# A decoder layer with two attentions: probabilities times values in three split passes, one head's transposed probabilities in six slots

## The chip, the cores and the metric

The kernel runs on one core of a Trainium2 chip. The metric is the device time of one launch in microseconds (us); smaller is better.

## What is computed

One layer of a decoder trunk in float32: 512 rows (tokens) of 2048 channels. The part that the change touches is the mixer with two attentions of eight heads each, both with values of 128 columns:

```python
h = rms_norm(x, g_attn) * (1 + sc_a) + sh_a          # sc_a, sh_a from c @ w_ada
proj = h @ w_in                                      # q, k, v, indexer, latents, gates
# mixer A: 8 query heads over 2 key/value heads, 128 keys chosen per row by an indexer
p = softmax(where(valid, qg @ k_sel, -inf));  o_a = p @ v_sel
# mixer B: 8 heads, keys and values from a latent, causal
p = softmax(where(causal, q @ k, -inf));      o_b = p @ v
merged = sigmoid(gate_a) * (o_a @ w_pa) + sigmoid(gate_b) * (o_b @ w_pb)
x = x + gt_a * (merged @ w_o)
x = x + gt_f * conv_ffn(rms_norm(x, g_ffn) * (1 + sc_f) + sh_f)
```

## The kernel before

The 512 rows are four blocks of 128, called tb for rows, qb for queries and kc for keys. Nearly all large products run as **three split passes**: both operands are held as a pair hi + lo in the type float32r, and mm3 (lines 165 to 168) issues hi·hi, hi·lo and lo·hi into one bank. The helper split (lines 152 to 154) makes such a pair: ACT copies the source to hi, and DVE subtracts hi from the source to give lo. Weights come by DMA into the buffer raw and are split into whl (wtile, lines 145 and 146; from line 1090 on by lines 153 and 154).

The small attention products are plain float32 matmuls: queries times keys (line 1023 in mixer A, line 1366 in mixer B beside the split rotary part of line 638) and **probabilities times values** (line 813).

One head goes like this. attend_p, or the loop in attend_pair, fills a bank with the scores of a query block; soft does the softmax on DVE (lines 784, 786, 787) and ACT (785), for qb 3 down to 0. attend_pv then takes the key blocks kc 0 to 3: for each it transposes the probabilities of the query blocks kc to 3 on PE (line 805, 10 transposes per head) into a bank, and copies 512, 384, 256 or 128 columns to SBUF, for even kc on ACT (line 810), for odd kc on DVE (line 808). Four matmuls with these widths add into one bank (line 813), which lines 815 and 816 split into the pair that the next product takes.

SBUF is handed out in 81 slots of 128x512 float32. attend_bufs takes five slots for probabilities and five for their transposes, enough for two heads at once (quad cuts them by the head's number modulo two), and four for outputs. at_bank gives the four PSUM banks 4 to 7 in turn to scores, transposes and outputs.

Beside the attention runs filler work, so that PE has something to do while softmax is under way: in mixer A the gate projections (gate_steps through fill) and a stream of w_ada columns that DVE adds up (lines 856 and 858, after ada_load, which takes two slots a step from those that are free); in mixer B the projection w_pa (pa_block) and the next pair's key, value and query projections (up_pair). After the last pair load_gates runs sigmoids on ACT (lines 1420 and 1421) on gates that it loads.

The program is not run in the order in which it is written: an ordering pass puts each engine's instructions in a row by priority, by a few explicit rules (high_priority, issue_after) and by its own estimate of when operands are ready. On the chip every engine then works through its row in order. So an instruction that waits holds up all that stand behind it on its engine.

## Time and profile before

| | |
|---|---|
| runs | 2595.93, 2594.96, 2591.62 us; median 2594.96 |
| profiled execution | 2592.58 us, of which its span is 2590.8 us |
| PE | 2574.9 us busy, 99% of the span; granted clock 1.000 |
| DVE | 2176.5 us, 84% |
| ACT | 1240.8 us, 48% |
| POOL | 374.7 us, 14% |
| probabilities times values (line 813) | 437 to 595 us (mixer A) and 837 to 992 us (mixer B) |

PE is busy throughout. The end of a matmul record is modelled, and records of consecutive matmuls overlap, so the cost of one in a stream is the step from its start to the next start, not its length. A row of the timeline may merge several records of one line (x10).

### The profile page before, as it was taken

How to read it: one execution, taken by the hardware profiler on the slowest of the kernel's cores; microseconds unless marked ns; L12 is line 12 of the kernel's file. 1: busy time of each engine (PE TensorE's matmuls, PEld its weight loads, DVE VectorE, ACT ScalarE, POOL GpSimd, SP SyncE). 2: the span in 40 equal slices, each digit the busy share in tenths (PEclk: the TensorE clock that was granted, in tenths of full speed). 3: DMA queues.
4: the chain of work that ended last, by engine and by line, in shares of the span. 5: the costliest groups of instructions: out<-in, count | busy, mean ns of one | idle time of the engine just before them, and what ended most of it. 6: DMA issues, size and time to landing. Idle time of an engine off the chain costs nothing.

```text
span 2590.8 us, 45201 instructions
## 1 busy us (share of the span) xinstructions
PE 2574.9 (99%) x17392; PEld 2340.4 (90%) x17392; DVE 2176.5 (84%) x3487; ACT 1240.8 (48%) x1949; POOL 374.7 (14%) x671
## 2 busy tenths in 40 slices
PE   9999999999999999999999999999999999999999
PEld 8887787779998877888889999999999999999999
DVE  7977986788878767876979989999989998989887
ACT  6333444344445535322545555555555555665554
POOL 1000011010023223200100000000000024414120
PEclk9999999999999999999999999999999999999999
DMA  9953136655685579976424334433444358868663
GB/s 342 362 166 103 45 102 203 214 160 170 210 265 168 160 213 347 322 232 225 155 75 158 125 122 137 138 116 132 129 147 137 125 173 229 225 168 226 155 204 116
DMA packets 216444, 466.41 MB, mean 180 GB/s; under 512 B 23930, under 2 KB 65556, under 8 KB 216228
## 3 DMA queue, kind: packets, MB, share of 16 engines
q1 hardware_dynamic: 170404, 344.93, 41.9%
q0 software_dynamic: 45792, 118.59, 15.4%
q8 instruction: 136, 2.23, 0.3%
q14 instruction: 80, 0.66, 0.1%
q10 hardware_dynamic: 32, 0.01, 0.0%
HBM read 398.16 MB, written 65.27 MB: 179 GB/s over the span
## 4 chain that ended last, share of the span: by engine, by line
PE 94%; issue 2%; DMA 2%; DVE 1%; ACT 1%; POOL 0%; SPq 0%; POOLq 0%; ACTq 0%; DVEq 0%
PE bank L1218 18%; PE bank L1220 18%; PE bank L1219 18%; PE bank L166 12%; PE bank L168 12%; PE bank L167 12%; PE bank L813 1%; PE bank L1366 1%; DMA raw<-in_w_ada 1%; PE bank L805 0%; PE bank L349 0%; DMA slot<-in_x 0%; PE bank L638 0%; DMA slot<-in_w_ada 0%; PE bank L1023 0%
## 5 line engine op out<-in xcount | busy, mean ns | idle before, releaser
L1218 PE MATMUL bank<-slot,whl 128*128 128x256 f32 x3920 | 1098.4, 281 | 3.1 <-ACT slot L1099 1.2
L1219 PE MATMUL bank<-slot,whl 128*128 128x256 f32 x3920 | 1097.1, 281 | 0.0
L1220 PE MATMUL bank<-slot,whl 128*128 128x256 f32 x3920 | 1084.9, 281 | 2.2 <-DVE whl L154 2.2
L1218 PEld LDWEIGHTS bank<-slot,whl 128*128 128x128 f32 x3920 | 737.3, 188 | 5.5 <-ACT slot L1099 2.3
L1219 PEld LDWEIGHTS bank<-slot,whl 128*128 128x128 f32 x3920 | 739.2, 189 | 0.2
L1220 PEld LDWEIGHTS bank<-slot,whl 128*128 128x128 f32 x3920 | 731.3, 188 | 2.7 <-DVE whl L154 2.6
L154 DVE TENSOR_TENSOR whl<-raw,whl 128x1024 fp32r<-128x1024 f32 (+2 forms) x560 | 608.0, 1088 | 126.5 <-ACT whl L153 120.8
L153 ACT ACTIVATE whl<-raw 128x1024 fp32r<-128x1024 f32 (+2 forms) x560 | 530.7, 949 | 359.2 <-PE bank L1219 180.2
L145 ACT ACTIVATE whl<-raw 128x1024 fp32r<-128x1024 f32 (+4 forms) x182 | 187.4, 1032 | 361.5 <-PE bank L168 183.1
L1095 DVE TENSOR_TENSOR raw<-raw 128x1024 f32<-128x1024 f32 (+2 forms) x320 | 347.3, 1085 | 3.9 <-DMA raw<-in_w_ups 1.7
L146 DVE TENSOR_TENSOR whl<-raw,whl 128x1024 fp32r<-128x1024 f32 (+4 forms) x182 | 215.7, 1187 | 111.3 <-ACT whl L145 109.8
L167 PE MATMUL bank<-whl,slot 128*128 128x512 f32 (+2 forms) x768 | 295.2, 385 | 0.0
L168 PE MATMUL bank<-whl,slot 128*128 128x512 f32 (+2 forms) x768 | 294.1, 385 | 0.0
L166 PE MATMUL bank<-whl,slot 128*128 128x512 f32 (+2 forms) x768 | 290.1, 389 | 0.8 <-DVE slot L1330 0.7
L167 PE MATMUL bank<-slot,whl 128*128 128x512 f32 (+1 forms) x656 | 263.5, 402 | 0.0
L166 PE MATMUL bank<-slot,whl 128*128 128x512 f32 (+1 forms) x656 | 261.3, 405 | 0.7 <-ACT slot L1548 0.7
L168 PE MATMUL bank<-slot,whl 128*128 128x512 f32 (+1 forms) x656 | 257.5, 401 | 0.0
L1101 ACT ACTIVATE slot<-bank 128x256 f32<-128x256 f32 x192 | 73.6, 383 | 210.9 <-PE bank L1220 210.9
L166 PEld LDWEIGHTS bank<-whl,slot 128*128 128x128 f32 x768 | 144.2, 188 | 30.5 <-issue 2.2
L858 DVE SCALAR_TENSOR_TENSOR slot<-slot,c_act,slot 128x512 f32<-128x512 f32 x203 | 151.0, 747 | 23.2 <-DMA slot<-in_w_ada 21.0
L167 PEld LDWEIGHTS bank<-whl,slot 128*128 128x128 f32 x768 | 144.4, 188 | 28.8 <-issue 2.1
L168 PEld LDWEIGHTS bank<-whl,slot 128*128 128x128 f32 x768 | 144.2, 188 | 28.9 <-issue 1.4
(302 smaller groups left out, 2789.7 us busy)
## 6 DMA issues: line engine op xcount, KB each, us to landing
slot<-in_w_ada SPq DMA_DIRECT2D x344, 256.0 KB, 5.4
raw<-in_w_ups SPq DMA_DIRECT2D x160, 512.0 KB, 3.7
raw<-in_w_in SPq DMA_DIRECT2D x50, 512.0 KB, 3.7
raw<-in_w_down SPq DMA_DIRECT2D x64, 384.0 KB, 4.0
raw<-in_w_down SPq DMA_DIRECT2D x64, 320.0 KB, 4.0
slot<-f POOLq DMA_DIRECT2D x154, 128.0 KB, 4.7
f<-slot POOLq DMA_DIRECT2D x66, 256.0 KB, 5.1
raw<-in_w_gs SPq DMA_DIRECT2D x32, 512.0 KB, 4.5
```

The lines of the kernel that those rows point to most:

```text
L145: A.activation(hi, raw[:, :w], AF.Copy)
L146: last["lo"] = V.tensor_tensor(lo, raw[:, :w], r32(hi), ALU.subtract)
L153: return (A.activation(dst_hi, src, AF.Copy), V.tensor_tensor(dst_lo, src, r32(dst_hi), ALU.subtract))
L154: V.tensor_tensor(dst_lo, src, r32(dst_hi), ALU.subtract))
L166: PE.matmul(o, lh, rh, start=first, stop=False)
L167: PE.matmul(o, lh, rl, start=False, stop=False)
L168: PE.matmul(o, ll, rh, start=False, stop=last)
L858: V.scalar_tensor_tensor(acc, ts[i], c_act[:, k:k + 1], acc, op0=ALU.mult, op1=ALU.add)
L1095: V.tensor_tensor(o[:, :W], a[:, :W], b[:, :W], op)
L1218: PE.matmul(o, wh[:, ks], rh, start=first and k == 0, stop=False, skip_group_check=True)
L1219: PE.matmul(o, wh[:, ks], rl, start=False, stop=False, skip_group_check=True)
L1220: PE.matmul(o, wl[:, ks], rh, start=False, stop=last, skip_group_check=True)
```

## The change

Probabilities times values becomes three split passes too.

- In attend_pv all four copies become split: ACT writes hi and DVE writes lo, for every kc, and the matmul becomes mm3.
- The transposed probabilities lie in three slots for hi and three for lo, of **one** head: quad is called with number 0 for each head. Before, there were five slots for two heads.
- The values are split too. In mixer A, four splits of 128x256 behind the key work of lines 714 to 722, into four new slots (va); the slots kva are given back earlier. In mixer B, line 1295 becomes a split, and vv takes four slots a pair instead of two.

```diff
--- before.py
+++ after.py
@@ -710,6 +710,10 @@
     qaT = {}
     kaT = [get(), get()]
     kva = part["B"][0:4]
+    va = ([getr(), getr()], [getr(), getr()])
+
+    def va_part(e, tb):
+        return va[e][tb // 2][:, (tb % 2) * 256:(tb % 2) * 256 + 256]
 
     for tb in range(4):
         t = kva[tb]
@@ -720,12 +724,14 @@
         rsqrt_mean(r, ss, P, 2)
         V.tensor_tensor(k3, k3, r[:, :, None].to_broadcast([P, 2, P]), ALU.mult)
         rope(k3, 2, 32, "ka", tb)
+        split(va_part(0, tb), va_part(1, tb), t[:, 256:512])
 
     for g in range(2):
         b = at_bank()
         for tb in range(4):
             PE.transpose(b[:, tb * P:(tb + 1) * P], kva[tb][:, g * P:(g + 1) * P], ident)
         A.activation(kaT[g], b, AF.Copy, scale=gk_col)
+    put(*kva)
 
     def ev_qa(cb):
         def ev(tb, b):
@@ -764,10 +770,11 @@
 
     def attend_bufs():
         att["p"] = [get() for _ in range(5)]
-        att["t"] = [get() for _ in range(5)]
+        att["t"] = [getr() for _ in range(3)]
+        att["l"] = [getr() for _ in range(3)]
         att["o"] = [getr() for _ in range(4)]
 
-    def attend_free(kinds="pto"):
+    def attend_free(kinds="ptlo"):
         for k in kinds:
             put(*att[k])
 
@@ -789,28 +796,25 @@
     def attend_p(qk, maskf, nsc, vf, dh, dl):
         i = hcount[0] % 2
         hcount[0] += 1
-        pq, pt = quad(att["p"], i), quad(att["t"], i)
+        pq = quad(att["p"], i)
         for qb in (3, 2, 1, 0):
             S = (qb + 1) * P
             b = at_bank()
             qk(b, qb, S)
             soft(b[:, :S], pq[qb][:, :S], maskf(qb), nsc(qb))
-        return i, pq, pt, vf, dh, dl
-
-    def attend_pv(i, pq, pt, vf, dh, dl):
+        return i, pq, vf, dh, dl
+
+    def attend_pv(i, pq, vf, dh, dl):
+        pt, pl = [quad([*att[n][0:2], None, None, att[n][2]], 0) for n in "tl"]
         for kc in range(4):
             b = at_bank()
             n = (4 - kc) * P
             for qb in range(kc, 4):
                 PE.transpose(b[:, (qb - kc) * P:(qb - kc + 1) * P], pq[qb][:, kc * P:(kc + 1) * P], ident)
-            d = pt[3 - kc]
-            if kc % 2:
-                last["cp"] = V.tensor_copy(d, b[:, :n])
-            else:
-                A.activation(d, b[:, :n], AF.Copy)
+            last["cp"] = split(pt[3 - kc], pl[3 - kc], b[:, :n])[1]
         ob = at_bank()
         for kc in range(4):
-            PE.matmul(ob[:, kc * P:], vf(kc), pt[3 - kc], start=kc == 0, stop=kc == 3)
+            mm3(ob[:, kc * P:], *vf(kc), pt[3 - kc], pl[3 - kc], kc == 0, kc == 3)
         oh, ol = att["o"][2 * i], att["o"][2 * i + 1]
         A.activation(oh, ob, AF.Copy)
         last["ol"] = V.tensor_tensor(ol, ob, r32(oh), ALU.subtract)
@@ -1023,7 +1027,7 @@
                 PE.matmul(o[:, :S], qaT[qb, g][:, (hd % 4) * P:(hd % 4 + 1) * P], kaT[g][:, :S], start=True, stop=True)
 
             state = attend_p(qk, lambda qb: mask[qb], lambda qb, hd=hd: nsc_a[:, qb, hd:hd + 1],
-                             lambda kc, g=g: kva[kc][:, 256 + g * P:256 + (g + 1) * P], *oa_d[hd])
+                             lambda kc, g=g: [va_part(e, kc)[:, g * P:(g + 1) * P] for e in range(2)], *oa_d[hd])
         fill(1, 1)
         if prev:
             attend_pv(*prev)
@@ -1031,7 +1035,7 @@
         prev = state
     fill(26)
     put(*kaT)
-    put(*kva)
+    put(*va[0], *va[1])
     for t in qaT.values():
         put(t)
     put(mslot, tslot[0])
@@ -1280,7 +1284,7 @@
 
     def up_pair(hp):
         kn = [get() for _ in range(2)]
-        vv = [get() for _ in range(2)]
+        vv = [getr() for _ in range(4)]
         kr = get()
         kr3 = kr.rearrange("p (t a d) -> p t a d", t=4, a=2)
 
@@ -1292,7 +1296,7 @@
             b4 = b.rearrange("p (n e d) -> p n e d", n=2, e=2)
             k3 = two(kn, tb)
             A.activation(k3, b4[:, :, 0, :], AF.Copy)
-            V.tensor_copy(two(vv, tb), b4[:, :, 1, :])
+            split(two(vv[0:2], tb), two(vv[2:4], tb), b4[:, :, 1, :])
             ss = sm.tile([P, 2], F32, name="ss2")
             head_ss(ss, k3, tb)
             V.tensor_scalar(ss, ss, ss_kr[:, tb:tb + 1], None, op0=ALU.add)
@@ -1366,7 +1370,7 @@
                 PE.matmul(bs[a][:, :S], qT[a][:, qs], kT[a][:, :S], start=False, stop=True)
                 soft(bs[a][:, :S], pq[a][qb][:, :S], Z[:, 384 - qb * P:512], nsc_b[:, qb, a:a + 1])
         for a in range(2):
-            attend_pv(a, pq[a], quad(att["t"], a), lambda kc, a=a: two(vv, kc)[:, a, :],
+            attend_pv(a, pq[a], lambda kc, a=a: [two(vv[2 * e:2 * e + 2], kc)[:, a, :] for e in range(2)],
                       *(ob_d[hp * 2 + a] if hp < 3 else (None, None)))
         put(*vv)
         put(*kT)
@@ -1390,7 +1394,7 @@
         pa_block(hp)
         if hp < 2:
             up_pair(hp + 2)
-    attend_free("pt")
+    attend_free("ptl")
 
     ada_in_slots[0] = ada_ring_on[0] = True
     ada_ring.extend(get() for _ in range(6))
```

The new rows have the line numbers of the changed file: transposes are L813 there (L805 before), the passes L166 to L168 with a slot on both sides, the copies and subtractions of split L153 and L154, sigmoids L1424 and L1425.

**PE, first pair of mixer B,** the end of the transposes and the start of probabilities times values; L813 below is the product before and the transpose after. Before:

```order
L805 MATMUL bank_73<-ident,slot_7244 128x128
L805 MATMUL bank_73<-ident,slot_7243 128x128
L168 MATMUL bank_68<-whl,slot_6540 128x384
L166 MATMUL bank_66<-whl,slot_446 128x384
L167 MATMUL bank_66<-whl,slot_446 128x384
L168 MATMUL bank_66<-whl,slot_447 128x384
L166 MATMUL bank_67<-whl,slot_6543 128x384
L813 MATMUL bank_70<-slot_7246,slot_6745 128x512
L813 MATMUL bank_70<-slot_7247,slot_6745 128x384
L813 MATMUL bank_70<-slot_7250,slot_6746 128x256
L813 MATMUL bank_70<-slot_7247,slot_6746 128x128
L813 MATMUL bank_71<-slot_7248,slot_6745 128x512
```

After:

```order
L813 MATMUL bank_73<-ident,slot_7356 128x128
L813 MATMUL bank_73<-ident,slot_7355 128x128
L166 MATMUL bank_70<-slot_5106,slot_847 128x512
L167 MATMUL bank_70<-slot_7359,slot_847 128x512
L168 MATMUL bank_70<-slot_5106,slot_852 128x512
L166 MATMUL bank_70<-slot_5107,slot_847 128x384
L167 MATMUL bank_70<-slot_7360,slot_847 128x384
L168 MATMUL bank_70<-slot_5107,slot_852 128x384
L166 MATMUL bank_70<-slot_7358,slot_851 128x256
L167 MATMUL bank_70<-slot_7361,slot_851 128x256
L168 MATMUL bank_70<-slot_7358,slot_6851 128x256
```

Five filler matmuls between the last transposes and the product are gone, and further up those between the transposes: between the last scores (128 columns) and the product there were 44 filler matmuls and are now 3. Behind these rows come the three passes of 128 columns and at once those of the second head.

**DVE, the same place,** from the row that finishes the last probabilities of the first head (128x128; ri is the reciprocal of the row sums). Before:

```order
L787 TENSOR_SCALAR slot_7242<-slot_7242,ri 128x128
L1295 COPY slot_6845<-bank_67 128x256
L1298 TENSOR_SCALAR ss_7528<-ss_7528,ss_kr 128x2
L787 TENSOR_SCALAR slot_7244<-slot_7244,ri 128x128
L707 TENSOR_REDUCE ss_7547<-slot_6726 128x2
L858 SCALAR_TENSOR_TENSOR slot_354<-raw,c_act,slot_354 128x512
L269 TENSOR_SCALAR rsm<-ss_7528 128x2
L1295 COPY slot_6999<-bank_68 128x256
L1298 TENSOR_SCALAR ss_7547<-ss_7547,ss_kr 128x2
L707 TENSOR_REDUCE ss_7566<-slot_6725 128x2
L858 SCALAR_TENSOR_TENSOR slot_354<-raw,c_act,slot_354 128x512
L808 COPY slot_7247<-bank_73 128x128
```

After:

```order
L794 TENSOR_SCALAR slot_7354<-slot_7354,ri 128x128
L154 TENSOR_TENSOR slot_7360<-bank_71,slot_5107 128x384
L793 RECIPROCAL ri<-su 128x1
L1305 TENSOR_TENSOR slot_7213<-slot_7213,rs_7712 128x256
L794 TENSOR_SCALAR slot_7356<-slot_7356,ri 128x128
L146 TENSOR_TENSOR whl<-raw,whl 128x1024
L154 TENSOR_TENSOR slot_7361<-bank_72,slot_7358 128x256
L154 TENSOR_TENSOR slot_7360<-bank_73,slot_5107 128x128
L154 TENSOR_TENSOR slot_7359<-bank_70,slot_5106 128x512
```

The lo parts of the four key blocks stand with a weight subtraction of 1024 columns (L146) among them, and the product waits for the last (512 columns).

**ACT, last pair of mixer B,** from the load of the sigmoid's table. Before:

```order
L1420 ACT_TABLE_LOAD
L1420 ACTIVATE slot_8828<-slot_8828 128x512
L810 ACTIVATE slot_7250<-bank_70 128x256
L1421 ACTIVATE slot_8820<-slot_8820 128x512
L810 ACTIVATE slot_7246<-bank_72 128x512
L1421 ACTIVATE slot_8829<-slot_8829 128x512
L810 ACTIVATE slot_7248<-bank_73 128x512
L1420 ACTIVATE slot_6746<-slot_6746 128x512
L810 ACTIVATE slot_7250<-bank_71 128x256
```

After:

```order
L1424 ACT_TABLE_LOAD
L1424 ACTIVATE slot_9216<-slot_9216 128x512
L1425 ACTIVATE slot_9217<-slot_9217 128x512
L153 ACTIVATE slot_7358<-bank_70 128x256
L153 ACTIVATE slot_5107<-bank_71 128x128
L1424 ACTIVATE slot_9225<-slot_9225 128x512
L153 ACTIVATE slot_5106<-bank_72 128x512
L1425 ACTIVATE slot_9226<-slot_9226 128x512
L1424 ACTIVATE slot_9234<-slot_9234 128x512
L1425 ACTIVATE slot_9235<-slot_9235 128x512
L153 ACTIVATE slot_5106<-bank_73 128x512
L153 ACTIVATE slot_5107<-bank_70 128x384
```

The copies of probabilities stand between sigmoids in both; after, all four of a head are there, and each has a subtraction on DVE behind it.

## Rows read from the trace of the kernel before

**Rows 1.** The page: busy time by engine, and the chain that ended last.
```profile
PE 2574.9 (99%) x17392; PEld 2340.4 (90%) x17392; DVE 2176.5 (84%) x3487; ACT 1240.8 (48%) x1949; POOL 374.7 (14%) x671
...
PE 94%; issue 2%; DMA 2%; DVE 1%; ACT 1%; POOL 0%; SPq 0%; POOLq 0%; ACTq 0%; DVEq 0%
```

**Rows 2.** Busy time by stage: start:end, length, PE, PEld, DVE, ACT, POOL, PEclk, DMA.
```profile
260.00:380.00 120.00, 120.00 (x623) 95.81 (x622) 113.02 (x306) 54.72 (x100) 13.32 (x11) 1.00 0.25 71
380.00:420.00 40.00, 40.00 (x182) 32.48 (x181) 15.55 (x23) 14.35 (x24) 6.47 (x12) 1.00 0.45 134
437.00:595.00 158.00, 156.96 (x696) 121.98 (x695) 125.94 (x261) 60.86 (x118) 16.13 (x30) 1.00 0.63 195
760.00:992.00 232.00, 231.08 (x1153) 182.53 (x1152) 167.86 (x490) 112.89 (x245) 77.16 (x113) 1.00 0.66 210
```

**Rows 3.** Probabilities times values (L813): timeline of PE (start, us long).
```profile
980.17 3.18 PE L813 MATMUL bank<-slot,slot 128*128 128x512 f32 x10
...
983.41 0.39 PE L168 MATMUL bank<-slot,whl 128*128 128x512 f32 x1
```

**Rows 4.** Timeline of PE: passes of 512, 384, 256, 128 columns, transposes (last: by form).
```profile
829.73 0.39 PE L168 MATMUL bank<-whl,slot 128*128 128x512 f32 x1
...
830.88 0.39 PE L167 MATMUL bank<-whl,slot 128*128 128x512 f32 x1
...
836.40 0.34 PE L167 MATMUL bank<-whl,slot 128*128 128x384 f32 x1
...
837.45 0.34 PE L167 MATMUL bank<-whl,slot 128*128 128x384 f32 x1
...
1499.83 0.29 PE L1219 MATMUL bank<-slot,whl 128*128 128x256 f32 x1
...
1500.77 0.28 PE L1218 MATMUL bank<-slot,whl 128*128 128x256 f32 x1
...
827.67 0.55 PE L638 MATMUL bank<-slot,slot 64*128 64x128 f32 x6
...
496.62 0.49 PE L805 MATMUL bank<-ident,slot 128*128 128x128 f32 x3
...
L805 PE MATMUL bank<-ident,slot 128*128 128x128 f32 x160 | 25.8, 272 | 0.1
```

**Rows 5.** DVE in the first pair of mixer B, and its weight split by form.
```profile
829.82 0.69 DVE L154 TENSOR_TENSOR slot<-slot,slot 128x512 fp32r<-128x512 f32 x1
...
830.43 0.35 DVE L784 CUSTOM_DVE_ANT_0 slot<-bank,slot,nsc_b 128x128 f32<-128x128 f32 x1
...
830.70 0.42 DVE L1295 COPY slot<-bank 128x256 f32<-128x256 f32 x1
...
831.03 0.55 DVE L808 COPY slot<-bank 128x384 f32<-128x384 f32 x1
...
832.60 0.28 DVE L787 TENSOR_SCALAR slot<-slot,ri 128x128 f32<-128x128 f32 x1
...
L146 DVE TENSOR_TENSOR whl<-raw,whl 128x1024 fp32r<-128x1024 f32 x43 | 52.3, 1220 | 14.7 <-ACT whl L145 14.4 <-PE bank L168 0.3
```

**Rows 6.** ACT in the last pair of mixer B.
```profile
974.03 1.28 ACT L1420 ACT_TABLE_LOAD   x1
975.71 0.63 ACT L1420 ACTIVATE slot<-slot 128x512 f32<-128x512 f32 x1 [0.39 <-DMA slot<-gate]
976.24 0.37 ACT L810 ACTIVATE slot<-bank 128x256 f32<-128x256 f32 x1
977.00 0.64 ACT L1421 ACTIVATE slot<-slot 128x512 f32<-128x512 f32 x1 [0.39 <-DMA slot<-gate]
```

**Rows 7.** Mixer A: DVE held by a transfer, PE behind it; total of such holds.
```profile
479.53 0.75 DVE L858 SCALAR_TENSOR_TENSOR slot<-slot,c_act,slot 128x512 f32<-128x512 f32 x1 [3.11 <-DMA slot<-in_w_ada]
...
483.41 0.49 PE L813 MATMUL bank<-slot,slot 128*128 128x128 f32 x2 [1.04 <-DVE slot L808]
...
  DMA slot<-in_w_ada: 9.5, 8
```

## The prediction

> **What bounds the kernel now.** I read the page's busy times first, then its chain of waits, then the stages of the change, then the order in time inside them. PE is busy for 2574.9 of 2590.8 us and makes up 94% of the chain that ended last [rows 1]: whatever PE does for less time is time won, as long as nothing new makes it wait. In the stages of the change PE is busy for 156.96 of 158 us in mixer A and 231.08 of 232 us in mixer B, at the full clock of 2.4 GHz (PEclk 1.00), while DVE has 32 and 64 us to spare there and ACT more [rows 2]. So the change is to be costed on PE, and its price is whatever wait its longer chain through ACT and DVE puts in front of PE.
>
> **What PE saves.** A float32 matmul of this product leaves two records. Ten of them, five matmuls with 1792 columns (a head's four and the next head's first), begin at 980.17; the second record of the three-pass stream behind them starts at 983.41, so the first at one step of 0.23 earlier, 983.18: 3.01 us [rows 3]. That is 1.68 ns a column, and a head with 512 + 384 + 256 + 128 = 1280 columns costs 2.15 us. The three passes are plain in the stream beside it [rows 4]: 512 columns step by (830.88 - 829.73) / 5 = 0.23 us, 384 by (837.45 - 836.40) / 6 = 0.175, 256 by (1500.77 - 1499.83) / 8 = 0.118. No row has a pass of 128 columns on the whole array. The nearest are transposes of 128 columns (three last 0.49 and one 0.272, so 0.11 a step) and split passes of 64 rows, three pairs in 0.55, less a tail of 0.27 and over two steps 0.14; halving the step of 256 gives 0.06. I take 0.11: the transposes are the nearest, with as many columns on as many rows, and every matmul has its weight load, 17392 of each [rows 1]. A head then costs 3 x (0.23 + 0.175 + 0.118 + 0.11) = 1.90 us. The gain is no quarter, because two records of float32 are not four passes: 0.25 us a head, mostly from the wide blocks; the block of 128 columns loses (0.33 against 0.22). Sixteen heads: **-4.0 us** (from -2.6 with 0.14 a step to -6.4 with 0.06).
>
> The order holds two more runs of the 64-row passes (20 against 18) and one fewer of the indexer's (24 against 25). The three pairs take 0.05 us more than transposes in their place would (0.55 against 0.49); with as much on leaving, and more where wider passes stand beside it, a run costs 0.1 to 0.3 us. I take the upper end, **+0.3 us**.
>
> One rule of the Trainium skill would make more of this. TensorE: Matmul & The Clock Gate, section Back-to-back issue gap, gives a step of columns / 2.4 + 2.5 ns at full clock; three passes of a head would be 1.63 us by it and the sixteen heads win 8.3 us. That is an estimate from the page, and this trace does not agree with it: 512 columns step by 0.23 us and not by 0.216 [rows 4].
>
> **What ACT and DVE get on top.** A head's copies were 512 and 256 on ACT, 384 and 128 on DVE; now each engine does all four. DVE steps by 0.61 us for a subtraction of 512 and 0.33 for a copy of 256, 0.08 less than they last, so by 0.47 for 384 [rows 5]; it gains 0.61 + 0.33 = 0.94 us a head, 15 us in all, and ACT about as much. The value splits of mixer A (four of 128x256, 1.3 us of DVE) stand in the stage from 260 us on where DVE has 113 of 120 us filled; PE does not see it, because the next 40 us have 24 us of DVE left and the masks are needed only after them [rows 2]. If that cover were gone it would cost the 1.3 us. In mixer B a subtraction takes the place of a copy of the same size, and ACT has 119 of 232 us free: nothing. No transfer is added, and the queues of SP and POOL carry the same ones.
>
> **Where PE will wait.** Before, two heads had separate slots for transposed probabilities. Now the second head's copies wait until the first head's product has read them. In mixer A that changes nothing: a head's transposes come after the product of the head before, and the order has some 20 filler matmuls (4.6 us) between transposes and product. In mixer B two heads come together, and the order shows where PE stands bare.
>
> First pair: 3 filler matmuls instead of 44 between last scores and product. From the row that finishes the first head's last probabilities, DVE has to do 384 (0.47), a reciprocal (about 0.07), a product of 256 (0.33), the second head's last probabilities (0.28 long, so 0.2), the weight subtraction of 1024 columns (1.22 long, so 1.14), 256 (0.33), 128 (0.2) and 512 (0.61): 3.35 us [rows 5]. PE has 13 transposes meanwhile, 1.4 us. So 1.9 us of wait. Before that stands softmax of the last 128 columns: 2.2 us from line 784 at 830.43 to line 787 at 832.60 for the second head [rows 5], for which PE has 3 filler matmuls and 6 transposes, 1.35 us; the first head's is somewhat earlier, so 0.6. And 0.2 when the second head's first block waits for ACT and DVE behind the first head's. I take **2.7 us**, between 0 (DVE is early, as in rows of before, where PE had no such wait) and 4.
>
> Last pair: every hi copy now stands between sigmoids. From the table load to the lo part that the product needs there are 1.28 us, two gaps of 0.39 for transfers, three sigmoids with a step of 0.53, copies of 256 and 128 (0.6) and of 512 (0.5), and DVE's 0.61 [rows 6]: 5.4 us, against 19 filler matmuls and 16 transposes, 6.1 us, in PE's row. That is about even. But the second head's last block has only one matmul between transpose and product, and three sigmoids (1.6 us) stand before its copy: **1.2 us**, between 0 and 4 if the gates come later. Second pair: **0.3 us** for the same reason as in the first with two filler matmuls; third pair: 21 filler matmuls, nothing.
>
> **Sum:** -4.0 + 0.3 + 2.7 + 1.2 + 0.3 = +0.5 us. The profiled execution took 2592.58 us (span 2590.8 and 1.8 around it), 2.4 below the median of 2594.96; 2593.1 on it, **2595.5 us** as a median. A measurement of this kernel tells 0.2%, 5.2 us, from no change: the edges are 2589.8 and 2600.2.
>
> **Rivals.**
>
> *The waits are covered.* PE's row is only an order; if DVE is ahead of what the ordering pass reckoned, the bare places cost nothing. For it: the trace has no wait of PE in the first and last pair of before. It could also take away the wait of 1.04 us in mixer A [rows 7]. Against it: before had the filler. Sum -4.0 + 0.3 - 1.04 = -4.7, 2590.2 us, still inside 0.2%. Chance 0.20.
>
> *The narrow passes run at column speed.* From 512 to 256 columns a step falls by 0.112, 0.44 ns a column; if that holds down to 128, the step is 0.06 and not 0.11, and 48 passes win 2.4 us more. With the waits covered that is -7.1, 2587.9 us: faster. The section of the Trainium skill named above points this way too. Against it stands the 0.11 of the transposes [rows 4]. Chance 0.10, with the tail of the first rival.
>
> *DVE is held in mixer A, and the product behind it* (the slower side). DVE works in order, and additions of the w_ada stream wait on their transfers in its row: eight times, 9.5 us in all. Once DVE stood for 3.11 us, and PE then waited 1.04 us for a copy of probabilities [rows 7]. The change makes both ends worse. Attention takes one slot more, so that counted along the program 4 or 3 slots are free when a step asks for two, where 5 or 4 were: a load can start only when the addition before the last is over. And all four blocks now need DVE, behind ACT. The chain of copies and subtractions is about 2.3 us of the 4.6 us of filler, so the point from which it decides is a hold of over 2.3 us. At 1 us for each of eight heads it is +0.5 + 8 = 2603.5 us. Against it: DVE has 32 us to spare in that stage, and the ordering pass knows the fewer slots. Chance 0.25, with other unlooked-for waits.
>
> *That the change does not do what it says* can be left out: all sixteen heads have their three passes in PE's row.
>
> **How the numbers follow.** The forecast has 0.45, the covered case 0.20; both lie inside 0.2%, so "same" has 0.65, "slower" 0.25 and "faster" 0.10. The range goes from 2589.5 (the covered case and a little of the narrow passes) to 2604 (the slower rival at its price), and leaves out about 2 in 10 on both sides together.
>
> **What would show it.** Line 166 to 168 with slots on both sides should step by 0.23, 0.175, 0.118 and 0.11 us in mixers A and B, a head's product should take 1.9 us; PE's waits should name the subtraction of line 154 and the copy of line 153 in the first and last pair of mixer B, with some 2 to 3 and 1 us; mixer A should be shorter by about 2 us, with no wait over 1 us. The forecast is wrong if narrow passes step by 0.06 or by 0.2, if PE waits over 1 us a head in mixer A, or if a stage that the change does not touch moves by over 2 us.

## The result, and the profile after

The changed kernel takes 2613.87 us (median of four runs, 2609.28 to 2616.07), the kernel before beside it 2593.29 (2590.93 to 2595.93): a ratio of 1.0076 with a 95% interval of 1.0064 to 1.0089. It is 20 us slower, where 0.5 us was forecast, and lies outside the range. The profiled execution took 2613.69 us, of which the span is 2611.9. (One run of a kernel below, adds_pool, took 5889.78 us and stands apart from all others; its median there is that of the other five.)

The page after, busy time and chain; [rows 1] are the same lines of before:

```profile
PE 2582.8 (99%) x17456; PEld 2352.9 (90%) x17456; DVE 2192.0 (84%) x3523; ACT 1255.0 (48%) x2001; POOL 365.3 (14%) x671
...
PE 91%; DMA 5%; DVE 2%; issue 1%; ACT 1%; POOL 0%; SPq 0%; DVEq 0%; POOLq 0%; ACTq 0%
```

PE's part of the chain fell from 94 to 91%, and transfers have 5% instead of 2. By stage, first after (mixer A, mixer B, what follows), then the last of these stages before; the others of before are in [rows 2]:

```profile
437.00:595.00 158.00, 157.34 (x736) 126.95 (x735) 130.72 (x277) 67.69 (x135) 16.16 (x30) 1.00 0.59 185
760.00:992.00 232.00, 222.81 (x1122) 178.90 (x1121) 168.92 (x493) 111.38 (x257) 57.94 (x91) 0.99 0.58 185
992.00:1100.00 108.00, 102.57 (x437) 82.06 (x436) 90.84 (x138) 48.35 (x75) 34.02 (x61) 0.97 0.95 324
```

```profile
992.00:1100.00 108.00, 108.00 (x467) 87.40 (x466) 98.74 (x143) 43.91 (x62) 25.24 (x45) 1.00 0.96 329
```

Mixer A is as before. In mixer B and behind it PE now stands for 9.2 + 5.4 us, where before it stood for 0.9, and the granted clock is below 1. The waits of PE from 806 to 1030 us after (in all, times, longest); before, the same question has no row at all:

```profile
PE bank L813 <- DVE mn L791: 3.6, 1, 3.6
PE bank L166 <- DVE slot L154: 2.3, 3, 1.6
PE bank L168 <- DVE whl L146: 2.0, 1, 2.0
PE bank L813 <- DVE slot L794: 1.4, 2, 0.8
PE bank L166 <- DVE slot L918: 1.4, 1, 1.4
```

Nearly all of them are waits for DVE. They lie in two stretches.

**The first pair of mixer B.** PE after, from the last transposes that still had filler to the second head's product (L813 is a transpose; L166 to L168 with a slot on both sides are the passes):

```profile
833.40 0.55 PE L813 MATMUL bank<-ident,slot 128*128 128x128 f32 x3 [0.62 <-DVE slot L794]
...
838.24 0.94 PE L813 MATMUL bank<-ident,slot 128*128 128x128 f32 x3 [3.60 <-DVE mn L791]
839.96 2.17 PE L813 MATMUL bank<-ident,slot 128*128 128x128 f32 x8 [0.77 <-DVE slot L794]
842.48 1.33 PE L813 MATMUL bank<-ident,slot 128*128 128x128 f32 x5 [0.35 <-DVE slot L154]
...
843.96 0.39 PE L167 MATMUL bank<-slot,slot 128*128 128x512 f32 x1
844.19 0.40 PE L168 MATMUL bank<-slot,slot 128*128 128x512 f32 x1
...
845.07 0.28 PE L167 MATMUL bank<-slot,slot 128*128 128x256 f32 x1
845.19 0.28 PE L168 MATMUL bank<-slot,slot 128*128 128x256 f32 x1
845.31 0.22 PE L166 MATMUL bank<-slot,slot 128*128 128x128 f32 x1
845.37 0.28 PE L167 MATMUL bank<-slot,slot 128*128 128x128 f32 x1
845.48 0.27 PE L168 MATMUL bank<-slot,slot 128*128 128x128 f32 x1
847.36 0.50 PE L166 MATMUL bank<-slot,slot 128*128 128x512 f32 x1 [1.61 <-DVE slot L154]
```

DVE in the same stretch (L862 adds w_ada columns, L791 is softmax, L146 the weight split, L154 a lo part):

```profile
834.93 0.75 DVE L862 SCALAR_TENSOR_TENSOR slot<-raw,c_act,slot 128x512 f32<-128x512 f32 x1 [1.58 <-DMA raw<-in_w_ada]
...
836.19 0.74 DVE L862 SCALAR_TENSOR_TENSOR slot<-raw,c_act,slot 128x512 f32<-128x512 f32 x1
...
837.83 0.34 DVE L791 CUSTOM_DVE_ANT_0 slot<-bank,slot,nsc_b 128x128 f32<-128x128 f32 x1
...
840.88 1.21 DVE L146 TENSOR_TENSOR whl<-raw,whl 128x1024 fp32r<-128x1024 f32 x1
842.01 1.20 DVE L154 TENSOR_TENSOR slot<-bank,slot 128x256 fp32r<-128x256 f32 x3
...
845.95 0.75 DVE L862 SCALAR_TENSOR_TENSOR slot<-raw,c_act,slot 128x512 f32<-128x512 f32 x1 [1.94 <-DMA raw<-in_w_ada]
846.62 0.68 DVE L154 TENSOR_TENSOR slot<-bank,slot 128x512 fp32r<-128x512 f32 x1
```

PE's 3.60 us end when DVE has done the first step of the softmax of the last 128 columns (L791, which reads the scores out of their bank). That stood behind an addition which waited 1.58 us for its transfer, a second addition and three reductions. The 1.61 us at the second head have the same cause: an addition that waited 1.94 us stands in DVE's row just ahead of the lo part.

The transposes at 838 and 840 us are slow by themselves: three take 0.94 us where three took 0.55 at 833.40. The windows show the granted clock (the figure behind POOL's busy time):

```profile
830.00:840.00 10.00, 5.01 (x28) 3.22 (x26) 8.22 (x37) 6.72 (x23) 2.65 (x4) 0.85 0.61 180
840.00:850.00 10.00, 8.04 (x43) 6.85 (x43) 7.99 (x20) 3.98 (x11) 1.28 (x2) 0.81 0.28 83
850.00:860.00 10.00, 10.00 (x58) 9.41 (x57) 8.54 (x38) 5.99 (x15) 3.07 (x5) 1.00 0.37 119
990.00:1000.00 10.00, 9.27 (x53) 7.72 (x52) 3.91 (x8) 8.52 (x17) 6.62 (x13) 1.00 1.01 382
1000.00:1010.00 10.00, 7.35 (x25) 5.17 (x24) 7.14 (x13) 5.89 (x10) 6.04 (x13) 0.83 1.06 386
1010.00:1020.00 10.00, 7.95 (x27) 6.03 (x27) 8.12 (x12) 3.04 (x6) 5.30 (x10) 0.83 1.05 387
```

The granted clock fell in the idle 3.60 us: PE began again at the lower level of 1.2 GHz, and by 850 us it ran at 2.4. From 830 to 850 us PE stood for 4.99 + 1.96 us, and its 16 transposes took some 2.1 us more than at full clock.

**The last pair and the start of w_pb.** PE after (L910 and L911 are the flush of the w_ada sums; L166 with whl is w_pb):

```profile
1000.66 0.50 PE L910 MATMUL bank<-slot,ones_r 128*128 128x512 f32 x1 [0.24 <-ACT slot L153]
...
1002.41 0.50 PE L911 MATMUL bank<-slot,ones_r 128*128 128x512 f32 x1 [0.82 <-DVE slot L154]
1004.27 0.80 PE L166 MATMUL bank<-slot,whl 128*128 128x512 f32 x1 [1.36 <-DVE slot L918]
1004.86 0.63 PE L167 MATMUL bank<-slot,whl 128*128 128x512 f32 x1
1005.29 0.63 PE L168 MATMUL bank<-slot,whl 128*128 128x512 f32 x1
...
1013.99 0.50 PE L168 MATMUL bank<-slot,whl 128*128 128x512 f32 x1 [2.05 <-DVE whl L146]
```

The flush is a chain of its own: a split of the sums on ACT and DVE, two matmuls, an evacuation on DVE (L918), and then w_pb writes into the same bank. Before, its second matmul (L907 there) ran with filler around it and nothing waited:

```profile
990.15 0.39 PE L907 MATMUL bank<-slot,ones_r 128*128 128x512 f32 x1
990.38 0.39 PE L168 MATMUL bank<-slot,whl 128*128 128x512 f32 x1
```

Now the filler is used up. Behind the waits of 1.36 and 2.05 us the passes of 512 columns step by 0.43 us (1004.86 to 1005.29), which is the lower clock, instead of 0.23: sixteen of them, from 1004.27 to 1007.79 and from 1014.56 to 1017.97, are some 3 us longer by it. The 2.05 us are a wait for weights, whose subtraction on DVE (1.22 us, from 1012.72) stands behind five products of the gates:

```profile
1009.70 3.10 DVE L1427 TENSOR_TENSOR slot<-slot,slot 128x512 f32<-128x512 f32 x5
```

A third difference is on POOL, whose queue loads the gates. Before, then after (in each, a store of pa and the first load for w_pb, which stands behind it):

```profile
967.89 0.55 POOL L947 DMA_DIRECT2D pa<-slot  x1 [6.44 <-ACT slot L946]
969.22 0.54 POOL L1415 DMA_DIRECT2D slot<-pa  x1 [0.77 <-PE bank L638]
```

```profile
983.90 0.54 POOL L951 DMA_DIRECT2D pa<-slot  x1 [4.49 <-ACT slot L950]
...
985.30 0.54 POOL L1419 DMA_DIRECT2D slot<-pa  x1
```

These loads take slots that the last pair's scores give back (before, the first waits for L638), and stand in POOL's row behind stores. The last scores are 17.3 us later, the first load is 16.1 us later, and the transfers' share from 980 to 990 us is 0.66 (before 1.01).

Where the time went, in us against the same event of the kernel before:

| event (before, at) | changed | a_only | b_alone | adds_pool | null_put | after_put |
|---|---|---|---|---|---|---|
| first matmul of the gate product behind mixer A (598.69) | -2.3 | -3.8 | +1.4 | -2.5 | -0.8 | -4.0 |
| last transposes of queries in mixer B (908.79) | +11.8 | -0.8 | +13.1 | +3.3 | -1.6 | +12.9 |
| last rotary scores (968.75) | +17.3 | -0.9 | +18.6 | +4.0 | +0.8 | +19.1 |
| first transposes behind w_o (1176.34) | +20.8 | -0.9 | +21.3 | +10.4 | +0.4 | +19.0 |

The other columns are runs of the next section.

### The profile page after: what moved, and what is told of

It is laid out like the page before. It is cut to its first block, busy times and chain, and to the rows that moved or that the text cites. A ratio compares the mean times of both kernels' runs of the same rounds, so it can differ in the third digit from the quotient of the medians.

```text
span 2611.9 us, 45454 instructions
## 1 busy us (share of the span) xinstructions
PE 2582.8 (99%) x17456; PEld 2352.9 (90%) x17456; DVE 2192.0 (84%) x3523; ACT 1255.0 (48%) x2001; POOL 365.3 (14%) x671
## 4 chain that ended last, share of the span: by engine, by line
PE 91%; DMA 5%; DVE 2%; issue 1%; ACT 1%; POOL 0%; SPq 0%; DVEq 0%; POOLq 0%; ACTq 0%
PE bank L1222 18%; PE bank L1224 18%; PE bank L1223 18%; PE bank L166 12%; PE bank L168 11%; PE bank L167 11%; DMA raw<-in_w_ada 2%; DMA slot<-in_w_ada 2%; DVE slot L862 1%; PE bank L1370 1%; PE bank L813 0%; DVE whl L146 0%; DMA slot<-in_x 0%; DMA slot<-gate 0%; PE bank L1027 0%
## 5 line engine op out<-in xcount | busy, mean ns | idle before, releaser
L154 DVE TENSOR_TENSOR whl<-raw,whl 128x1024 fp32r<-128x1024 f32 (+2 forms) x560 | 607.6, 1088 | 122.4 <-ACT whl L153 117.7
L153 ACT ACTIVATE whl<-raw 128x1024 fp32r<-128x1024 f32 (+2 forms) x560 | 530.6, 949 | 367.5 <-PE bank L1223 184.2
L146 DVE TENSOR_TENSOR whl<-raw,whl 128x1024 fp32r<-128x1024 f32 (+4 forms) x182 | 215.7, 1186 | 106.2 <-ACT whl L145 104.8
L168 PE MATMUL bank<-whl,slot 128*128 128x512 f32 (+2 forms) x768 | 293.7, 384 | 0.0
L166 PE MATMUL bank<-whl,slot 128*128 128x512 f32 (+2 forms) x768 | 289.3, 388 | 1.9 <-DVE slot L154 1.4
L166 PE MATMUL bank<-slot,whl 128*128 128x512 f32 (+1 forms) x656 | 260.2, 404 | 2.3 <-DVE slot L918 1.4
L168 PE MATMUL bank<-slot,whl 128*128 128x512 f32 (+1 forms) x656 | 257.6, 402 | 2.0 <-DVE whl L146 2.0
L862 DVE SCALAR_TENSOR_TENSOR slot<-slot,c_act,slot 128x512 f32<-128x512 f32 x203 | 151.2, 747 | 35.5 <-DMA slot<-in_w_ada 33.8
L166 PEld LDWEIGHTS bank<-whl,slot 128*128 128x128 f32 x768 | 144.0, 188 | 31.1 <-issue 1.7
L168 PEld LDWEIGHTS bank<-whl,slot 128*128 128x128 f32 x768 | 144.3, 188 | 29.8 <-issue 2.2
```

Source lines behind the costliest of these rows:

```text
L146: last["lo"] = V.tensor_tensor(lo, raw[:, :w], r32(hi), ALU.subtract)
L153: return (A.activation(dst_hi, src, AF.Copy), V.tensor_tensor(dst_lo, src, r32(dst_hi), ALU.subtract))
L154: V.tensor_tensor(dst_lo, src, r32(dst_hi), ALU.subtract))
L166: PE.matmul(o, lh, rh, start=first, stop=False)
L168: PE.matmul(o, ll, rh, start=False, stop=last)
L862: V.scalar_tensor_tensor(acc, ts[i], c_act[:, k:k + 1], acc, op0=ALU.mult, op1=ALU.add)
```

## The experiments

Eighteen kernels; medians in us, ratios to runs of the kernel before on the same chip.

| run | median | ratio (95%) |
|---|---|---|
| a_only | 2594.53 | 1.0005 (0.9995 to 1.0014) |
| b_alone | 2616.94 | 1.0093 (1.0078 to 1.0108) |
| share_only | 2604.26 | 1.0049 (1.0034 to 1.0064) |
| gates_behind | 2610.99 | 1.0075 (1.0059 to 1.0092) |
| no_val_lo | 2599.80 | 1.0021 (1.0011 to 1.0030) |
| no_prob_lo | 2607.52 | 1.0053 (1.0035 to 1.0070) |
| adds_behind | 2634.95 | 1.0153 (1.0136 to 1.0170) |
| no_flush | 2616.78 | 1.0092 (1.0074 to 1.0110) |
| null_s80 / after_s80 | 2610.17 / 2627.44 | 1.0062 (1.0047 to 1.0077) / 1.0134 (1.0119 to 1.0149) |
| before_no_adds / no_adds_first | 2608.14 / 2616.16 | 1.0059 (1.0043 to 1.0074) / 1.0092 (1.0076 to 1.0108) |
| before_ticks_moved / ticks_moved | 2604.86 / 2613.18 | 1.0046 (1.0031 to 1.0062) / 1.0074 (1.0061 to 1.0087) |
| null_put / after_put | 2596.39 / 2609.40 | 1.0015 (1.0005 to 1.0024) / 1.0061 (1.0044 to 1.0077) |
| ticks_early | 2626.79 | 1.0127 (1.0113 to 1.0141) |
| adds_pool | 2604.21 | 1.0052 (1.0039 to 1.0065) |

**Which mixer.** a_only gives attend_bufs and attend_pv a flag `three` that is false in mixer B; there the copies, the float32 product, the five slots and the unsplit values are those of before. b_alone is the reverse.

> The change in mixer A alone; mixer B as before (float32 product, copies on ACT and DVE, five slots for two heads). PE's row in mixer B is the one of the kernel before. Theory (all of the loss comes from mixer B and its end, mixer A is shorter by what three passes save): 2 to 2.5 us faster than before, ratio 0.9990 to 0.9993, no fall of the granted clock. Rival (the new value slots and the tighter slots of mixer A move something later): as slow as the whole change or part of it, 5 us or more over before.

> The change in mixer B alone; mixer A as before. PE's row in mixer B is the one of the changed kernel. Theory: 21 to 24 us slower than before, with the two stretches of waits (first pair, and last pair with the start of w_pb) and the half clock behind them as in the changed kernel. Rival (the loss needs both parts, by the slots that mixer A hands on): under 12 us slower.

b_alone has the whole loss, in the same two stretches. a_only has none, but no gain either: from its first scores to the first matmul of the gate product mixer A takes 175.2 us instead of 178.4, and by the start of mixer B 3.0 us of it are given back in the gate product between (PE is busy for 159.68 of its first 163 us, before for 160.88). Why it is given back there was not tested.

**One suspect at a time.** First the sharing alone, on the kernel before:

```diff
-        att["t"] = [get() for _ in range(5)]
+        att["t"] = [get() for _ in range(3)]
...
-        pq, pt = quad(att["p"], i), quad(att["t"], i)
+        pq, pt = quad(att["p"], i), quad([*att["t"][0:2], None, None, att["t"][2]], 0)
```

> The kernel before with the transposed probabilities of all heads in one set of three slots (the first two and the fifth), float32 product, copies on ACT and DVE as before, values not split. It has the sharing of the change and nothing else. Theory (the loss is the longer chain through ACT and DVE in rows where these engines are held up, and PE's row without filler): 0 to 4 us slower than before, since the row keeps its filler between transposes and products. Rival (sharing one head's slots is the cause: the second head's copies wait for the first head's product): 10 us or more slower, with waits of PE in the second head of a pair.

It is some 12 us slower, which the theory did not allow; the size is the rival's. But the waits are not where the changed kernel has them: none in the first pair, one of 3.2 us in the third (transposes behind a copy on DVE) and 3.7 us for weights, 1.2 in w_pb and 2.5 in w_o. The copy stands in DVE's row behind an addition that waits for its transfer:

```profile
942.67 1.54 DVE L858 SCALAR_TENSOR_TENSOR slot<-raw,c_act,slot 128x512 f32<-128x512 f32 x2 [5.27 <-DMA raw<-in_w_ada]
```

The kernel before has the same hold, 4.89 us to 938.54, with no wait of PE behind it. So this run does not show that the sharing alone costs 12 us: its row is another one too. A kernel with the change and separate slots for two heads was not run.

Then sigmoids behind the last hi copy:

```diff
-            with tc.issue_after(last["exp"].ins):
+            with tc.issue_after(last["hi"].ins):
```

> The changed kernel with one bound moved: the sigmoids on the gates may start behind the last hi copy of the last pair instead of behind its last exponential. PE's row is the same up to the flush of the w_ada sums behind it. Theory (in the last pair every hi copy stands behind sigmoids that wait for their transfers, and the wait of PE behind them lets the granted clock fall): the stretch from 995 to 1020 us loses 2 to 5 us instead of 10.5, so 5 to 8 us faster than the changed kernel, 2606 to 2609 us. Rival (the last pair waits for DVE, whose row stays as it is, or for the shared slots): within 2 us of the changed kernel.

The rival was nearer. The last pair's own waits fall from 0.73 to 0.24 us, but those of the flush stay (1.87 us instead of 2.42), and w_pb's weights are then late by 1.34 and 2.47 us. Mixer B's first scores come 1.8 us earlier than the changed kernel's, and its profiled span is 2.4 us shorter.

Then one half of the split left out in mixer B: in no_val_lo line 1299 becomes a copy on DVE into two slots, in no_prob_lo the four split copies become ACT and DVE copies in turn; each has two passes.

> The changed kernel without the lo part of the values in mixer B: their copy on DVE as before, two slots a pair instead of four, and two passes (hi with hi, hi with the lo of the probabilities), so the third pass is left out and the output is less exact. The six shared slots and the split copies of the probabilities stay. PE's row has its cover back: in the first pair 17, 8 and 30 filler matmuls among the transposes where the changed kernel has 3, behind the last product 157. PE has 8 x 0.63 = 5.0 us less to do than in the changed kernel. Theory now (the loss is PE's row without filler at the first and the last pair): no wait over 1 us and no fall of the granted clock there, 2586 to 2594 us. Rival (the shared slots and the longer chain through ACT and DVE cost it, in whatever row): 2600 us or more.

> The changed kernel without the lo part of the probabilities in mixer B: four copies on ACT and DVE in turn, as before, and two passes (the lo with lo-free probabilities left out, so the output is less exact). The split of the values stays, and so does PE's bare row in the first pair (3 filler matmuls, then 16 transposes and the products) and behind the last product (107). PE has 5.0 us less to do than in the changed kernel and the chain through ACT and DVE is as short as before. Theory (the bare row is the cause): 6 us or more of waits in the first pair all the same, 2600 to 2607 us. Rival (the longer chain is the cause): 2588 to 2594 us.

no_val_lo came out at the rival's edge (2599.80, where that said 2600 or more), no_prob_lo half a us above its theory's range. With the row covered, no_val_lo has no wait over 0.84 us in the first pair, but still loses 6 us although PE has 5 us less to do, most of it in two waits of 3 us for flushes (PE waits for the evacuation, 6.1 us in all). no_prob_lo keeps the wait of 3.5 us for softmax in the first pair, without any lo part of the probabilities in the chain, and DVE there waits 1.49 us for the transfer of an addition; so that wait is indeed one of the row and of DVE's additions, not of the longer chain. It has the flush wait of 3.2 us too.

Then the additions and the flush themselves:

```diff
+            elif not ada_in_slots[0] and "cp" in last:
+                st.enter_context(tc.issue_after(last["cp"].ins))
```

> The changed kernel with the additions of the w_ada stream in mixer B ordered behind the latest subtraction of transposed probabilities that is written ahead of them, so that an addition that waits for its transfer no longer stands in DVE's row between the softmax of a pair and its products. PE's row is still bare in the first pair (19 transposes, then the products). Theory (in the first pair DVE is held by these additions): the first pair loses 5 us or less instead of 10.5, the end of the run is 5 us or more ahead of the changed kernel, 2603 to 2609 us. Rival (DVE is late by its own work, or another hold takes the place): within 2 us of the changed kernel.

```diff
-        if cb == 0:
-            flush_cols(bk[3])
```

> The changed kernel without the early flush of the w_ada sums ahead of w_pb (its two matmuls, the split ahead of them and the evacuation come later, with the next flush; the sums are the same). PE's row is the same up to the last pair and has filler there again: 13 more matmuls among the transposes, 36 instead of 21 behind them, and the flush behind 9 more of the row. Theory (in the last pair PE waits through that flush: split on ACT and DVE, two matmuls, evacuation on DVE, and only then the next matmul into the same bank, with the half clock behind it): 5 to 9 us faster than the changed kernel, 2604 to 2609 us, and the first pair loses its 10 us as before. Rival (sigmoids, products on DVE and late weights hold the start of w_pb by themselves): within 3 us of the changed kernel.

Both failed by their times, because another hold took the place. In adds_behind the wait of 3.60 us for softmax is gone: up to the first pair's last products no wait of PE is over 0.51 us, which speaks for the additions having held it. But held additions keep the buffers raw, which weights use too, and PE then waits for weights, 7.76 us of it soon behind the first pair (waits of PE from 806 to 1200 us):

```profile
PE bank L166 <- ACT whl L145: 23.7, 4, 7.8
```

Without the early flush PE runs on to the next thing that is late, the heads that are loaded back from DRAM (no_flush, 806 to 1030 us):

```profile
PE bank L167 <- DMA slot<-obl: 3.4, 1, 3.4
PE bank L166 <- DMA slot<-obh: 2.3, 1, 2.3
```

**Edits without operations, and the change in pairs.** After this it was open whether the loss is the change's operations or the row that the ordering pass lays anew around them. So the kernel before got edits that add no operation, and the changed kernel the same ones: 80 slots instead of 81; the w_ada stream at rest in the first block of w_pa; the same with the other three blocks a third faster; and the slots of a finished pair given back in the opposite order.

```diff
-    n_slots=81,
+    n_slots=80,
...
-        lin_fm(w_pa, cb * 512, oa, 8, MM, ev_store(pa_d, cb * 4), tick=ticker(TP))
+        lin_fm(w_pa, cb * 512, oa, 8, MM, ev_store(pa_d, cb * 4), tick=ticker(TP) if cb else None)
...
+        lin_fm(w_pa, cb * 512, oa, 8, MM, ev_store(pa_d, cb * 4), tick=ticker(TP * 4 / 3) if cb else None)
...
-        put(*vv)
-        put(*kT)
-        put(*qT)
         put(*kTr, *qTr)
+        put(*qT)
+        put(*kT)
+        put(*vv)
```

> The kernel before with 80 slots instead of 81: not one operation is added or removed; only the numbers of the slots that are handed out, and with them the ordering pass's row in mixer B, are others. Theory (a row of mixer B that the ordering pass lays anew costs time by itself, because its clock does not know the transfers and holds of the chip): 3 to 12 us slower than before, in waits of PE between 800 and 1030 us. Rival (what costs time are the operations that the change adds): within 2 us of before.

> The changed kernel with 80 slots instead of 81, to stand beside the kernel before with 80 (2610.2 us). Theory: 5 to 11 us slower than that, 2615 to 2621 us. Rival (20 us in any row): 2625 us or more.

> The kernel before with the w_ada stream at rest during the first block of w_pa, nothing else. Theory: its row has filler with and without these additions, so 2590 to 2597 us, no difference that can be told from none; it shows what of the run with the whole change and this edit is due to the edit. Rival (the stream's additions in the first pair cost the kernel before too): 4 us or more faster than before.

> The whole change, with the w_ada stream at rest during the first block of w_pa (its five steps come later; everything is computed). DVE has no addition that waits for a transfer in the first pair, and PE's row has filler at both places: 15, 3, 8 and 6 matmuls among the transposes of the first pair, 92 between the last pair and the flush. Six shared slots, split copies, value splits and three passes all stay. Theory (the operations of the change cost nothing on PE's path where its row has filler): no wait over 1 us and no fall of the clock in mixer B, 2588 to 2595 us, which is before or up to 5 us better. Rival (the longer chain through ACT and DVE and the shared slots cost it in whatever row): 2602 us or more.

> The kernel before with the same move of the w_ada stream and nothing else. Theory: no operation is added, its row in the first pair was covered already; last scores at 968 to 972 us and 208 to 213 us from there, 2592 to 2600 us. Rival (any row that the ordering pass lays anew costs some ten us): 2603 us or more.

> The whole change, with the w_ada stream at rest during the first block of w_pa and a third faster during the other three, so that w_pb's stage gets no more of it than in the changed kernel. Theory now: the first pair loses its 10 us to the stream's additions ahead of softmax on DVE and PE's row without filler; and the end of the last pair's scores releases the slots into which gates, w_pb's weights' neighbours and w_ada are loaded, so that from there to the first transposes behind w_o a fixed 208 to 213 us pass, with the transfers at their full rate. So: first pair without a wait over 1 us, last scores at 966 to 971 us (before: 969, changed kernel: 986), 2592 to 2599 us. Rival (the waits of the last pair come from the longer chain through ACT and DVE): last scores early, but 10 us lost behind them, 2602 us or more.

> The kernel before with the slots of a finished pair given back in the opposite order (rotary keys and queries first, values last): no operation, no size and no number of slots changes, only which slot is handed out next, and so the ordering pass's row in mixer B. Theory (a good part of the loss is that the row of the kernel before is a lucky one, which any such edit loses): 5 to 16 us slower than before. Rival (the other edits of the kernel before cost what they cost by the slot or the stream that they moved): within 3 us of before.

> The changed kernel with the same opposite order of giving back. In its row the first pair has filler (24 and 27 matmuls among the transposes) and so has the last (83 ahead of the flush). Theory (the operations of the change cost about 8 us in rows of the same origin, as in the two pairs with the w_ada stream moved: 2616.2 against 2608.1 and 2613.2 against 2604.9): 5 to 11 us slower than the kernel before with this edit. Rival (the change costs its 20 us in any row): 15 us or more slower than that kernel.

The edits alone cost the kernel before 0.62, 0.59, 0.46 and 0.15%, which is 16, 15, 12 and 4 us. The first takes a slot away and the next two move transfers, so that only null_put, which changes nothing but the slot that is handed out, is the price of a row by itself: 4 us. Within each pair the kernel with the change is slower by 0.72, 0.33, 0.28 and 0.46%, and without an edit by 0.76%: 19, 9, 7, 12 and 20 us. It is slower every time, clear of noise. But the ordering pass lays the change's row anew in every pair, so each difference holds the operations and a row together. In the pair with 80 slots 7.6 of the 19 us are there at the first scores of mixer B (819.7 against 812.1 us), where the change in mixer A alone costs nothing; in the first pair with the stream moved (before_no_adds and no_adds_first) the changed kernel is 2.3 us ahead at the last scores and loses its time behind them. What the operations cost by themselves is not shown; that a row without them costs 4 us, and with less room or moved transfers up to 16, is.

What the operations do is plainest in the waits for lo parts of probabilities and values, which only kernels with the change have. after_put has filler among the transposes of its first pair and still waits (PE, 806 to 1030 us):

```profile
PE bank L166 <- DVE slot L154: 9.1, 4, 4.0
```

null_put beside it has one wait, of 1.7 us, in the same stretch, at full clock. null_s80, though, waits 3.2 us for the evacuation of the flush (PE L166 for DVE L914) without one operation of the change, so that this wait can come with a row alone. Of the 9.1 us 2.65 are a projection that waits for the lo part of values; the longest, 3.95 us, is the product of the first pair. DVE reaches its lo part of 512 columns late:

```profile
845.41 0.75 DVE L862 SCALAR_TENSOR_TENSOR slot<-raw,c_act,slot 128x512 f32<-128x512 f32 x1 [0.77 <-DMA raw<-in_w_ada]
...
848.21 2.35 DVE L146 TENSOR_TENSOR whl<-raw,whl 128x1024 fp32r<-128x1024 f32 x2
850.48 0.68 DVE L154 TENSOR_TENSOR slot<-bank,slot 128x512 fp32r<-128x512 f32 x1
```

In no_adds_first mixer B was nearly clean: 2.4 us of waits, and at the last scores it is 1.8 us ahead of before. That run's loss is all behind them, where the five steps of the stream that it put off are loaded with everything else (PE waits 5.9 us for obh and 3.6 for obl); before_no_adds loses its 15 us there as well. ticks_moved was to have both, and did not: its later pairs, with more additions in DVE's row, wait 9.6 us for lo parts.

> The kernel of the first run of this call, with five more steps of the w_ada stream taken in the gate projections ahead of mixer B (at 597 to 760 us, where the transfers are at two thirds of their rate) and none in w_pb's first block, where they are at their full rate. Theory (the stretch behind the last scores is bound by transfers): 2.6 MB less there at some 385 GB/s is up to 7 us, so it takes 201 to 209 us instead of 208 to 213 and the run 2587 to 2595 us. Rival (that stretch is bound by PE's own work, with the transfers just beside it): no faster than the first run of this call, by under 2 us.

ticks_early is ticks_moved with five more steps of the stream ahead of mixer B (TS 0.41 instead of 0.36) and none in w_pb's first block. It was the worst of those that move the stream: 8.5 us of waits for lo parts in mixer B, and from the last scores to the transposes behind w_o 224.8 us, 6.8 of them waits for obh and obl. The simple picture, that this stretch is bound by how many bytes are moved, does not hold. It takes 207 to 214 us in the other runs, but for the two whose stream was put off (223 and 232) and the one whose weights were held (238).

**The additions off DVE.** The last run keeps the change and every transfer of it, and does the additions of mixer B on POOL, each as a product and a sum (the first product of a sum, which has no addition, stays on DVE):

```diff
-                    V.scalar_tensor_tensor(acc, ts[i], c_act[:, k:k + 1], acc,
-                                           op0=ALU.mult, op1=ALU.add)
+                    if ada_in_slots[0]:
+                        V.scalar_tensor_tensor(acc, ts[i], c_act[:, k:k + 1], acc,
+                                               op0=ALU.mult, op1=ALU.add)
+                    else:
+                        G.tensor_scalar(ts[i], ts[i], c_act[:, k:k + 1], None, op0=ALU.mult)
+                        G.tensor_tensor(acc, acc, ts[i], ALU.add)
```

> The whole change, with the additions of the w_ada stream in mixer B done on POOL (a product and a sum) instead of DVE, at the same places of the stream; no transfer moves to another stage. DVE has some 20 x 1.4 = 28 us less to do in mixer B and no instruction in its row there that waits for a w_ada transfer. Theory (the change's own cost in mixer B is the wait for the lo parts and for softmax behind a DVE that is held by these additions): PE waits under 2.5 us for softmax and copies between 806 and 992 us (changed kernel 7.4), last scores at 965 to 973 us, from there 207 to 213 us to the first transposes behind w_o, 2592 to 2602 us. Rival (the chain is too long without any hold, or POOL, whose row has the loads of the gates behind these additions, starts them later): waits of 5 us or more there or more than 215 us behind the last scores, 2606 us or more.

2604.21 us: 13 us more than before, where the changed kernel has 20, so 6 to 8 us less (by the ratios and by the medians, each against the kernel before on its own chip); between theory and rival, so. Of the 17.3 us at the last scores 4.0 are left. The waits for lo parts are not gone (4.4 us in four), and behind the last pair stands the flush again (waits of PE, 806 to 1030 us):

```profile
PE bank L166 <- DVE slot L154: 4.4, 4, 1.7
PE bank L166 <- DVE slot L922: 3.2, 1, 3.2
```

This run's row is another one as well, so not all of these 6 to 8 us are shown to be DVE's relief.

## Why the prediction was wrong

**What PE saves: right.** The steps are 0.23 and 0.12 us for 512 and 256 columns (843.96 to 845.31 above) and 0.17 for 384, as forecast. Of 128 columns the first pass steps by 0.06 (845.31 to 845.37) and the second by 0.11, as the third does where other matmuls follow at once; so a head costs 1.85 us. The rival of narrow passes at column speed holds for one pass in three, 0.8 us in all, and falls for the other two. By its formula for a matmul by itself, the section Back-to-back issue gap of TensorE: Matmul & The Clock Gate in the Trainium skill would have given 0.216 us for 512 columns and 0.056 for 128. This trace does not agree with it at 512, and at 128 for the first pass alone.

**Mixer A: right in size, not in the sum.** It was to win 2 us and won 1.8 (176.7 us from first scores to gate product instead of 178.4), with no wait over 1 us. But the a_only run shows that this gain does not reach the end, and in the changed kernel the first scores of mixer B come only 0.2 us earlier than before. The forecast booked it as won because PE is busy 99% there.

**The first pair, "2.7 us, between 0 and 4": this step failed.** It measured some 9 us: 6.95 of idle PE and 2.1 by the clock. The place was right, the engine and the instructions too. What was mis-sized is DVE's part: I added up the chain's own instructions and took softmax of the last 128 columns, 0.6 us of wait, from rows of before. In DVE's row of the change, two w_ada additions and three reductions stand ahead of that softmax, and the first waits 1.58 us for its transfer; together they made it 3.60. In mixer B of before such additions wait 18.7 us in all for their transfers, ten times, and I had priced such waits for mixer A only. The rival "DVE is held in mixer A" had the mechanism, at 1 us a head and at the wrong place: in mixer A PE has filler behind it, in the first pair of mixer B it has none.

**The last pair, "1.2 us, between 0 and 4": this step failed too.** Measured are 5.4 us of idle PE from 990 to 1020 us and some 3 us by the clock. I looked at the sigmoids ahead of the hi copies. gates_behind took them away, and the end did not move. What waits there is the flush and the first weights of w_pb, which had filler ahead of them and now have not. The forecast followed PE's row to the last product and not beyond.

**Not in the sum at all: the granted clock.** After idle of 3.60 us, after 2.4 us in three pieces up to 1004.27, and after 2.05 us up to 1013.99, PE's rows are at the lower of its two levels, 1.2 GHz. The sixteen transposes of the first pair cost some 2.1 us more by it, and each of sixteen 512 steps of w_pb 0.2. Idle and clock of the two stretches are together some 18 us.

**Also not in it: the row.** That the queues carry the same transfers was true, but the gates' loads came 16 us later, since their slots come from the last scores and they stand behind stores. And the row of before was taken as the measure of what a row costs. null_put, which only hands out other slots, shows that it is a good one by 4 us; the three edits that also take a slot or move transfers cost 12 to 16.

What is left open: how much of the 20 us is the change's operations and how much its row; how the operations' part divides between six shared slots, the longer chain and the value split (all wait for DVE, and no run has separate slots); and why the ordering pass lays PE's first pair bare.

## What to carry to other kernels

Where a row is laid by an ordering pass, cost a change by the row that it gets: take each place where PE stands bare, list everything that stands ahead of the needed result on the engine that it waits for, with the waits of these instructions for transfers in it, and go on past the last changed instruction until PE has filler again. Compare the change with the kernel before in several rows (an edit that alters no operation gives one): what an empty edit costs is the row, and a difference within a pair is the change only as far as it is larger than that. A saving of 4 us of PE was worth nothing here beside a DVE that is held by additions waiting for transfers; of the edits of the changed kernel that leave out none of its work, taking these off DVE won the most, 6 to 8 of the 20 us.

## What was not expected of the hardware

Handing out the same 81 slots in another order costs 0.15% (null_put), one slot fewer 0.62%, with every operation the same; the order of the instructions changes with it, so that this is not shown to be the chip's doing. The clock fell with idle of 3.60 and of 2.05 us, while with a wait of 1.04 us in mixer A of before [rows 7], of 1.7 us in null_put and even of 3.17 us in share_only (at 946.26) it stayed at 1.00: the length of one wait does not tell whether it falls. And a pass of 128 columns steps by 0.06 us behind wider passes and by 0.11 behind another of 128.
